# A decoder trunk on one core: the last gates' weights ahead of the pages, and the output weights in the space of the head inputs

## The chip, the cores and the metric

The kernel runs on one core of one Trainium2 chip, in float32 throughout. The metric is device time in microseconds (us) of one execution; the time before is the median of three runs.

## What is computed

Two layers, A and B, are run with the same weights for a prompt of 512 rows and for a group of 8 sequences with 4 new rows each (32 "sample" rows). Layer A mixes by trailing means and a memory attention. Layer B, in which the change lies, has multi-head latent attention and a memory attention, both gated, one output projection and a final norm:

```python
z = h @ w_in_b[j]
c_q, gate_t, q_m, gate_m = jnp.split(z, [...], axis=-1)
tok = mla_mix(c_q, pos, ckv_all, krope_all, ...)
mem_o = mem_attend(q_m..., mem_k[l], mem_v[l])
mixed = jnp.concatenate([tok * silu(gate_t), mem_o * silu(gate_m)], axis=-1)
x = x + mixed @ w_out[l]
return rmsnorm(x, g_final), ...
```

For the prompt the attention is causal over 512 rows, head by head (8 heads of 128). For the sample rows it goes over 4096 cached rows per sequence, in pages of 128 rows of 320 numbers (256 latent, 64 rotary) that a page table names, and over the 4 new rows themselves. `gate_t` has 1024 columns (8 blocks of 128), `mixed` has 1536 (12 blocks), `w_out` is 1536x1024.

## The kernel before

Activations lie transposed: 128 columns of the model on the partitions, 544 rows (512 prompt and 32 sample) along them, worked in two halves of 272. A product in float32 is made of three matmuls on numbers rounded to a shorter float (`mm3`, L93 to L95; `mm3_late`, L99 to L101): each factor is split into a high part, cast by ACT (L88), and the rest, a subtraction (L89) on DVE or POOL. A weight block goes `wr` (as loaded, L208) to `wh` and `wl`. The pool `pw` holds three `wr` and two of each of `wh` and `wl`.

PE is the engine with most work. From the late gates on, PE's and SP's instructions run in the order in which the code issues them. That order comes from `weave`: it steps through a few generators ("threads"), always the one that is furthest behind its planned share. ACT, DVE and POOL are ordered by the scheduler.

The parts from there on, in time:

- `gates_late`: the gates of blocks 4 to 7 of `gate_t`, 48 matmuls of 128x272 each (`pa` and `po` are the halves' sums). Woven with it are the first rounds of the pages. `late_w` holds the loaded weights. The split is issued in the gate that uses it. The loads of blocks 4 and 5 are issued early, block 6 behind the first 16 pages, block 7 behind 32.
- Rounds (`round_scores`, `round_values`): each of the 8 sequences has 2 rounds of 16 pages. `load_half` reads eight page numbers into registers (L973) and issues eight page loads (L977, `nat`, four buffers) on SP. PE transposes the keys (L134, `tr`, copied to `kt` at L985), makes scores (L1020 with the latent part, L1029 with the rotary one), and takes the values (L1057, after `rt`).
- `heads` and `head_inputs`: the prompt's eight heads, woven with the rounds. Their inputs (`qh`, `ql`, `wuh`, `wul`, `kx`, `qr`, `q`), raw weights and probabilities are in one pool, `pat`.
- `out_all`: the output projection of the prompt. Twelve slabs (two column halves `fh` times six steps `s`) of `w_out` (128x2x512 each, L1446) are loaded and split by `prepare`; a slab has 24 matmuls of 128x512 into four banks `oa`. `mix_b` makes the split of a gated block of `mixed`: from SBUF for blocks 0 to 7, from DRAM (`gmd`, the memory outputs) for 8 to 11. `load_rest` issues the loads of the residual `x` and the last gains on POOL. The pool `fin`, opened when `pat` closes, holds both slabs and `x`.
- `sample_out`, woven with the second part of `out_all`: `combine` joins the rounds' partial results with the 4 own rows (the own scores are L1292 and L1295, tiny matmuls), then the sample rows' output projection (L1541) reads the same `w_out` slabs again (`ws`, three buffers).

The first three slabs are split on DVE, later ones on POOL:

```python
wh, wl = split(fin("wh", F32R), fin("wl", F32R), t, nc.gpsimd if (fh, s) > (0, 2) else nc.vector)
```

Of the kernel before, what the change touches and what calls it, by code (L numbers as in the profile page):

```python
# [37 lines left out]
def trunk_kernel(ctx: ExitStack, tc: tile.TileContext, A, O):  # L38
# [891 lines left out]
    def weave(threads, last):  # L930

        while not all(t.done for t in last):
# [349 lines left out]
    weave([rv, rs, ha, hi], [ha, hi])  # L1282
    pat.close()
    hb.close()


    def combine(cb):
        ps = ps_("tr")
        sv = ps[:NS, :NS].rearrange("p (b t) -> p b t", b=NB)
        for b in range(NB):  # L1290
            for k in range(2):
                nc.tensor.matmul(  # L1292
                    sv[:, b, :], lhsT=QT[:, k, b, :], rhs=ckT_s[:, k, b * NT : (b + 1) * NT], start=k == 0, stop=False
                )
            nc.tensor.matmul(  # L1295
                sv[:, b, :], lhsT=Qr[:64, b, 0, :], rhs=krT_s[:, b * NT : (b + 1) * NT], start=False, stop=True
            )
        w = cb("c")
        tail = w[:NS, :NS].rearrange("p (b t) -> p b t", b=NB)
        nc.vector.tensor_tensor(  # L1300
            out=tail,
            in0=sv,
            in1=cp[:NS, C_TMASK : C_TMASK + NT].unsqueeze(1).broadcast_to([NS, NB, NT]),
            op=ALU.add,
        )
        tst = w[:NS, 64:80]
        nc.vector.tensor_reduce(out=tst[:, :NB], in_=tail, axis=AX.X, op=ALU.max, negate=True)
        nc.vector.tensor_tensor(out=tail, in0=tail, in1=tst[:, :NB].unsqueeze(2).broadcast_to([NS, NB, NT]), op=ALU.add)
        nc.scalar.activation(w[:NS, :NS], w[:NS, :NS], AF.Exp)
        nc.vector.tensor_reduce(out=tst[:, NB:], in_=tail, axis=AX.X, op=ALU.add)  # L1310
        L = P + NS
        yield 0.5, 4.5
        ps = ps_("tr")
        transpose(ps[:NB, :P], stats_m)
        transpose(ps[:NB, P:L], tst[:, :NB], NS)
        transpose(ps[:NB, L : L + P], stats_s)
        transpose(ps[:NB, L + P : 2 * L], tst[:, NB:], NS)
        ms = cb("t")
        nc.vector.tensor_copy(ms[:NB, : 2 * L], ps[:NB, : 2 * L])
        m, s = ms[:NB, :L], ms[:NB, L : 2 * L]  # L1320
        m3 = m.rearrange("p (g c) -> p g c", c=NS)
        g = cb("c")
        mn, den, rec = (g[:NB, i * NS : (i + 1) * NS] for i in range(3))
        nc.vector.tensor_reduce(out=mn, in_=m.rearrange("p (g c) -> p c g", c=NS), axis=AX.X, op=ALU.min)
        nc.vector.tensor_tensor(out=m3, in0=mn.unsqueeze(1).broadcast_to([NB, 5, NS]), in1=m3, op=ALU.subtract)
        nc.scalar.activation(m, m, AF.Exp)
        nc.vector.tensor_tensor(out=s, in0=s, in1=m, op=ALU.mult)
        nc.vector.tensor_reduce(out=den, in_=s.rearrange("p (g c) -> p c g", c=NS), axis=AX.X, op=ALU.add)
        nc.vector.reciprocal(out=rec, in_=den)
        nc.vector.tensor_tensor(out=m3, in0=m3, in1=rec.unsqueeze(1).broadcast_to([NB, 5, NS]), op=ALU.mult)  # L1330
        yield 0.5, 4.5
        ps = ps_("tr")
        transpose(ps[:, :NB], m[:, :P], NB)
        transpose(ps[:NS, 16 : 16 + NB], m[:, P:L], NB)
        wn = cb("c")
        nc.vector.tensor_copy(wn[:, :NB], ps[:, :NB])
        nc.vector.tensor_copy(wn[:NS, 16 : 16 + NB], ps[:NS, 16 : 16 + NB])
        selw = cb("t")
        nc.vector.tensor_tensor(
            out=selw[:, :256].rearrange("p (c t) -> p c t", c=NB),  # L1340
            in0=sel.unsqueeze(1).broadcast_to([P, NB, NS]),
            in1=wn[:, :NB].unsqueeze(2).broadcast_to([P, NB, NS]),
            op=ALU.mult,
        )
        tz = cb("t")
        nc.vector.memset(tz[:NS, :288], 0.0)
        nc.vector.tensor_tensor(
            out=tz[:NS, :288].rearrange("p (b c) -> p b c", c=36)[:, :, :NT],
            in0=tail,
            in1=wn[:NS, 16 : 16 + NB].unsqueeze(2).broadcast_to([NS, NB, NT]),  # L1350
            op=ALU.mult,
        )
        yield 0.5, 4.5
        ps = ps_("tr")
        for b in range(NB):
            transpose(ps[:NS, b * NS : (b + 1) * NS], tz[:NS, b * NS : (b + 1) * NS], NS)
        tt = cb("t")
        nc.vector.tensor_copy(tt[:NS, :256], ps[:NS, :256])
        yield 0.5, 4.5
        po = ps_("tr")  # L1360
        for bq in range(2):
            for r in range(2):
                for b4 in range(4):
                    b = bq * 4 + b4
                    if r == 0:
                        lhsT, rhs = selw[:, b * NS : (b + 1) * NS], ostore[:, b, :]
                    else:
                        lhsT, rhs = tt[:NS, b * NS : (b + 1) * NS], ck_nat
                    nc.tensor.matmul(
                        po[b4 * NS : (b4 + 1) * NS, bq * 256 : (bq + 1) * 256],  # L1370
                        lhsT=lhsT,
                        rhs=rhs,
                        start=r == 0,
                        stop=r == 1,
                    )
        on = cb("t")
        nc.vector.tensor_copy(on, po)
        yield 0.5, 4.5
        ps = ps_("tr")
        for i in range(4):  # L1380
            transpose(ps[:, i * P : (i + 1) * P], on[:, i * P : (i + 1) * P])
        oT = cb("t")
        for bq in range(2):
            for k in range(2):
                c = (bq * 2 + k) * P
                nc.vector.tensor_copy(
                    oT[:, k * 256 : (k + 1) * 256].rearrange("p (h b t) -> p b h t", h=8, b=NB)[
                        :, bq * 4 : bq * 4 + 4
                    ],
                    ps[:, c : c + P].rearrange("p (b h t) -> p b h t", b=4, h=8),  # L1390
                )
        v = [cb("v") for k in range(2)]
        for k in range(2):
            src = A["w_v_up"][k * P : (k + 1) * P].rearrange("p h c -> p (h c)")
            tc.keep_in_program_order(nc.sync.dma_start(v[k], src))
        yield 0.5, 4.5
        po = ps_("tr")
        for h2 in range(2):
            for k in range(2):
                for j in range(4):  # L1400
                    h = h2 * 4 + j
                    nc.tensor.matmul(
                        po[j * NS : (j + 1) * NS, h2 * P : (h2 + 1) * P],
                        lhsT=oT[:, k * 256 + h * NS : k * 256 + (h + 1) * NS],
                        rhs=v[k][:, h * P : (h + 1) * P],
                        start=k == 0,
                        stop=k == 1,
                    )
        ov = cb("t")
        nc.vector.tensor_copy(ov[:, :256], po[:, :256])  # L1410
        yield 0.5, 4.5
# [287 lines left out]
```

## Time and profile before

| | |
|---|---|
| median of three runs | 892.81 us (890.89 to 894.15) |
| profiled execution | 890.33 us, of which span 888.6 |
| mean granted TensorE clock | 0.984 |
| PE busy | 831.5 us, 94% of the span |
| DVE, ACT, POOL busy | 515.5, 349.5, 250.0 us (58, 39, 28%) |
| DMA | 139.46 MB, mean 157 GB/s |
| chain that ended last | PE 71%, DVE 10%, issue 6%, DMA 5%, ACT 4% |

The profile is of one execution; times in it count from the span's start. A row of its timeline reads: start, duration, engine, line and operation, what it writes and reads, and in brackets how long the engine had been idle and what released it. SPq stands for SP issuing a DMA; the transfer lands some microseconds later. A row of its table by stage has for each engine the busy time and the number of instructions, then the granted clock of PE (1.00 is full), the busy share of the DMA engines and GB/s. Busy PE may still be PE at half clock, which only the clock's column tells.

### The profile page before, as it was taken

The numbers are of one execution on the slowest core, as the hardware profiler recorded it, in microseconds if no ns is written. First come the engines' busy times: TensorE is split into PE (matmuls) and PEld (weight loads), VectorE is DVE, ScalarE is ACT, GpSimd is POOL, SyncE is SP. The second block draws the span as 40 slices with busy tenths as digits, with TensorE's granted clock in tenths as the row PEclk, the third lists the DMA queues.
The fourth block names the chain that finished last, engine by engine and source line by source line (L and its number), as shares of the span: only waits on it lengthen the run. The fifth ranks groups of instructions, "written<-read, shape, count | busy, mean of one in ns | idle before, by whom it ended". The sixth has DMA issues, their size and how long they took to land.

```text
span 888.6 us, 18551 instructions
## 1 busy us (share of the span) xinstructions
PE 831.5 (94%) x7162; PEld 715.1 (80%) x7162; DVE 515.5 (58%) x964; ACT 349.5 (39%) x693; POOL 250.0 (28%) x203
## 2 busy tenths in 40 slices
PE   6999999889999999999999789989999899899996
PEld 6989989889999898779988766768778777666664
DVE  7666666987734456757665225575656656544312
ACT  7443333222433253353332225544545535432212
POOL 0043323533334134024232127240411300032420
PEclk9999999999999999999999889999999999998998
DMA  8355176321232436366265725646555455792344
GB/s 303 96 196 185 48 246 204 105 69 52 100 106 84 119 123 201 98 213 223 77 222 187 210 90 179 201 148 179 161 166 175 138 148 159 239 326 70 119 143 171
DMA packets 80858, 139.46 MB, mean 157 GB/s; under 512 B 9057, under 2 KB 49762, under 8 KB 80514
## 3 DMA queue, kind: packets, MB, share of 16 engines
q1 hardware_dynamic: 76258, 123.53, 44.1%
q0 software_dynamic: 4512, 14.75, 4.7%
q8 instruction: 56, 0.92, 0.4%
q14 instruction: 32, 0.26, 0.1%
HBM read 129.53 MB, written 8.72 MB: 156 GB/s over the span
## 4 chain that ended last, share of the span: by engine, by line
PE 71%; DVE 10%; issue 6%; DMA 5%; ACT 4%; POOL 2%; SPq 2%; POOLq 0%; DVEq 0%; ACTq 0%
PE pa L93 13%; PE pa L95 13%; PE pa L94 13%; PE tr L134 7%; PE ac L1020 3%; PE ac L1057 3%; POOL wl L89 2%; DVE v L582 2%; PE oa L93 2%; PE ac L1029 1%; PE oa L94 1%; PE oa L95 1%; SPq L977 1%; DVE t L744 1%; PE ac L388 1%
## 5 line engine op out<-in xcount | busy, mean ns | idle before, releaser
L93 PE MATMUL pa<-h,wh 128*128 128x272 f32 x832 | 242.0, 293 | 9.7 <-ACT wh L88 5.2
L95 PE MATMUL pa<-h,wl 128*128 128x272 f32 x832 | 239.6, 293 | 5.1 <-POOL wl L89 5.1
L89 POOL TENSOR_TENSOR wl<-wr,wh 128x1024 fp32r<-128x1024 f32 (+1 forms) x64 | 148.7, 2324 | 247.9 <-ACT wh L88 234.0
L94 PE MATMUL pa<-h,wh 128*128 128x272 f32 x640 | 186.0, 291 | 0.0
L93 PEld LDWEIGHTS pa<-h,wh 128*128 128x128 f32 x832 | 158.9, 191 | 14.4 <-ACT wh L88 5.7
L95 PEld LDWEIGHTS pa<-h,wl 128*128 128x128 f32 x832 | 157.7, 191 | 7.9 <-POOL wl L89 6.2
L88 ACT CAST wh<-wr 128x1024 fp32r<-128x1024 f32 (+1 forms) x87 | 87.7, 1008 | 165.7 <-PE pa L94 53.8
L94 PEld LDWEIGHTS pa<-h,wh 128*128 128x128 f32 x640 | 122.8, 192 | 0.9
L134 PE MATMUL tr<-c,nat 128*128 128x128 f32 x512 | 79.6, 280 | 8.1 <-DVE kt L987 3.9
L985 ACT COPY kt<-tr 128x512 f32<-128x512 f32 x86 | 50.2, 588 | 72.1 <-PE tr L134 70.6
L134 PEld LDWEIGHTS tr<-c,nat 128*128 128x128 f32 x512 | 59.3, 141 | 23.4 <-issue 7.3
L260 DVE SCALAR_TENSOR_TENSOR g<-t,g 128x272 f32<-128x272 f32 x48 | 48.0, 1006 | 17.1 <-ACT t L259 17.1
L94 PE MATMUL pa<-g,wh 128*128 128x272 f32 x192 | 54.5, 288 | 0.1
L259 ACT ACTIVATE t<-g 128x272 f32<-128x272 f32 x48 | 20.3, 429 | 75.8 <-DVE g L246 74.5
L987 DVE COPY kt<-tr 128x512 f32<-128x512 f32 x42 | 28.9, 687 | 26.9 <-PE tr L134 26.6
L246 DVE SCALAR_TENSOR_TENSOR g<-pa,r 128x272 f32<-128x272 f32 x42 | 18.1, 438 | 43.3 <-PE pa L95 43.2
L93 PE MATMUL oa<-wh,c 128*128 128x512 f32 x96 | 41.5, 432 | 0.0
L94 PE MATMUL oa<-wl,c 128*128 128x512 f32 x96 | 38.8, 405 | 0.6 <-POOL wl L89 0.6
L94 PEld LDWEIGHTS pa<-g,wh 128*128 128x128 f32 x192 | 36.1, 188 | 0.3 <-DVE g L89 0.3
L89 DVE TENSOR_TENSOR wl<-wr,wh 128x1024 fp32r<-128x1024 f32 x23 | 28.1, 1224 | 12.7 <-ACT wh L88 12.6
L1020 PE MATMUL ac<-kt,c 128*32 128x256 f32 x512 | 34.9, 384 | 0.0
L89 DVE TENSOR_TENSOR q<-q,q 128x512 fp32r<-128x512 f32 x16 | 25.2, 1574 | 11.2 <-ACT q L88 11.1
(365 smaller groups left out, 1710.9 us busy)
## 6 DMA issues: line engine op xcount, KB each, us to landing
nat<-in_cache_P SPq DMA_DIRECT2D x256, 160.0 KB, 3.1
wr<-in_w_in_a SPq DMA_DIRECT2D x24, 512.0 KB, 3.8
wr<-in_w_in_b SPq DMA_DIRECT2D x19, 512.0 KB, 3.7
cs<-in_mem_kT SPq DMA_DIRECT2D x16, 512.0 KB, 5.4
wr<-in_w_out_a SPq DMA_DIRECT2D x16, 384.0 KB, 3.1
wr<-in_w_out_b SPq DMA_DIRECT2D x12, 512.0 KB, 5.5
ws<-in_w_out_b SPq DMA_DIRECT2D x12, 512.0 KB, 4.9
wr<-in_w_mem_k SPq DMA_DIRECT2D x8, 512.0 KB, 3.8
```

What stands on the lines that cost most here:

```text
L88: nc.scalar.copy(h, src)
L89: (eng or nc.vector).tensor_tensor(out=l, in0=src, in1=fr(h), op=ALU.subtract)
L93: nc.tensor.matmul(out, lhsT=wh, rhs=xh, start=start, stop=False)
L94: nc.tensor.matmul(out, lhsT=wh, rhs=xl, start=False, stop=False)
L95: nc.tensor.matmul(out, lhsT=wl, rhs=xh, start=False, stop=stop)
L134: nc.tensor.transpose(out, in_, ident[:k, :k])
L259: nc.scalar.activation(th[:, :HALF], z[:, o : o + HALF], AF.Tanh)
L260: nc.vector.scalar_tensor_tensor(out=z[:, o : o + HALF], in0=th[:, :HALF], scalar=1.0, in1=z[:, o : o + HALF], op0=ALU.add, op1=ALU.mult,)
L985: nc.scalar.copy(out, src)
L987: nc.vector.tensor_copy(out, src)
L1020: nc.tensor.matmul(o[j * NS : (j + 1) * NS, :], lhsT=QT[:, k, b, :], rhs=kt[ih, j // 2, k][:, j % 2 * 256 : (j % 2 + 1) * 256], start=k == ...
L1057: nc.tensor.matmul(po[j * NS : (j + 1) * NS, :256], lhsT=pT[:, i * P + j * NS : i * P + (j + 1) * NS], rhs=nat[i // 2][:, 2 * j + i % 2, : ...
```

## The change

Three things are done.

1. **Late gates.** Blocks 6 and 7 of the weights are loaded ahead of all pages, and a block's split is issued when the gate before it begins (`late_s`).
2. **Pools.** `pat` becomes three pools: `heads_raw`, `heads_val` and `heads_in`. `heads_in` closes as soon as the last head is scored (`weave` may now end on a condition), while its values are still to be made. `fin`, now only `wr`, `wh` and `wl`, takes that space. `x` and the gains go to `fin2`, in the place of the pages' pool when that closes. Small tiles of the last part use tags of the remaining pools.
3. **Output stage.** All slabs are split on POOL. The own scores become a thread of their own (`own_scores`), woven with the last head's values. `prepare` of the next slabs follows each finished slab; only step 4 is put off to be done together with step 5 (before: 3 and 4). The own `ws` slabs have five buffers, and their matmuls come two slabs at a time. The blocks 8 to 11 are read into `tab`.

```diff
     def gates_late():
         for f in range(4, 8):
-            wh, wl = split_w(late_w.pop(0), KD, P, nc.gpsimd)
-            if f == 4:
-                late_w.append(load_w(wb[3 + 7], KD, P)[0])
+            wh, wl = late_s.pop(0)
+            if late_w:
+                late_s.append(split_w(late_w.pop(0), KD, P, nc.gpsimd))
...
-    late_w = [load_w(wb[3 + f], KD, P)[0] for f in (4, 5)]
-    load_half(0, 0)
-    load_half(0, 1)
-    late_w.append(load_w(wb[3 + 6], KD, P)[0])
-    for h in range(2, 4):
+    late_w = [load_w(wb[3 + f], KD, P)[0] for f in (4, 5, 6)]
+    late_s = [split_w(late_w.pop(0), KD, P, nc.gpsimd)]
+    late_w.append(load_w(wb[3 + 7], KD, P)[0])
+    for h in range(4):
         load_half(h // 2, h % 2)
...
-    pat = Pool(
-        "pat", "left", tab=(512, 2), qw=(384, 2), qh=(384, 2), ql=(384, 2), wu=(512, 2), wuh=(512, 2), wul=(512, 2),
-        vx=(D, 2), kx=(512, 4), qr=(512, 3), e0=(128, 1), e1=(256, 1), e2=(384, 1), e3=(512, 1), p=(512, 4), q=(512, 5),
+    heads_raw = Pool("hraw", "left", tab=(512, 2), qw=(384, 2), wu=(512, 2))
+    heads_val = Pool("hval", "left", e0=(128, 1), e1=(256, 1), e2=(384, 1), e3=(512, 1), p=(512, 4), vx=(D, 2))
+    heads_in = Pool(
+        "hin", "left", qh=(384, 2), ql=(384, 2), wuh=(512, 2), wul=(512, 2), kx=(512, 4), qr=(512, 3), q=(512, 5)
     )
...
-    weave([rv, rs, ha, hi], [ha, hi])
-    pat.close()
-    hb.close()
...
+    weave([rv, rs, ha, hi], lambda: hi.done and heads_scored[0] == 8)
+    heads_in.close()
+    fin = Pool("fin", "left", wr=(D, 3), wh=(D, 3), wl=(D, 3))
...
+        wh, wl = split(fin("wh", F32R), fin("wl", F32R), t, nc.gpsimd)
...
+    prepared = [prepare(*slabs.pop(0)) for _ in range(3)]
...
         late = []
         for s in range(6):
-            if fh == 0 and s == 2:
-                load_rest()
-            if slabs:
-                prepared.append(prepare(*slabs.pop(0)))
             wh, wl = prepared.pop(0)
             late.append((s, wh, wl))
-            if s in (3, 4):
+            if s == 4:
                 continue
...
+            for _ in late:
+                if slabs:
+                    prepared.append(prepare(*slabs.pop(0)))
             late = []
...
+    os_ = Thread(own_scores(), 1.0, 0.0, 1.0, now[0])
+    weave([rv, rs, ha, os_], [ha, os_])
+    hb.close()
+    hb = Banks(oa=4)
+    out = Thread(out_all(), 112 / total, 66 / total, 66.0, now[0])
+    weave([rv, rs, out], [rv, rs])
+    sp_order.__exit__(None, None, None)
+    nats.close()
+    fin2 = Pool("fin2", "right", x=(D, 4), g=(D, 1), gs=(256, 1))
+    cb = Pool("cb", "right", c=(96, 3), ws=(D, 5))
+    load_rest()
...
-    out = Thread(out_all(), 118 / total, 66 / total, 66.0, now[0] + 10.0)
-    weave([rv, rs, out], [rv, rs])
-    sp_order.__exit__(None, None, None)
-    nats.close()
-    cb = Pool("cb", "right", v=(D, 2), t=(512, 4), c=(96, 3), ws=(D, 3))
...
-        here = [slab(cb("ws"), *todo.pop(0)) for _ in range(3)]
+        here = [slab(cb("ws"), *todo.pop(0)) for _ in range(5)]
...
-                yield 0.44, 1.0
+                if s % 2:
+                    yield 0.88, 0.5
```

PE issues as many instructions as before. The numbers in a name count tiles; they differ between the two programs for the same thing. Where the instructions stand, at the three places that matter below:

SP at the late gates, before: `p` is the last memory values, `nat` a half round of pages, `wr_5777` the weights of gate 6.

```order
L425 DMA p_5545<-in_cache_mem_v 128x512
L425 DMA p_5546<-in_cache_mem_v 128x512
L425 DMA p_5557<-in_cache_mem_v 128x512
L425 DMA p_5558<-in_cache_mem_v 128x512
L977 ISA
L977 DMA nat_5613<-in_cache_P 128x320
...
L977 DMA nat_5695<-in_cache_P 128x320
L208 DMA wr_5777<-in_w_in_b 128x1024
L973 TENSOR_LOAD c_4072
L973 ISA x16
```

The same place after, where `wr_5613` is gate 6's weights and `wr_5619` gate 7's; a line number is one higher there.

```order
L208 DMA wr_5613<-in_w_in_b 128x1024
L425 DMA p_5545<-in_cache_mem_v 128x512
L208 DMA wr_5619<-in_w_in_b 128x1024
L974 TENSOR_LOAD c_4072
L974 ISA x4
L425 DMA p_5546<-in_cache_mem_v 128x512
L425 DMA p_5557<-in_cache_mem_v 128x512
L974 ISA x2
L425 DMA p_5558<-in_cache_mem_v 128x512
L974 ISA x10
L978 ISA
L978 DMA nat_5621<-in_cache_P 128x320
```

Both loads moved ahead of 32 page loads and stand among the `p` loads. ACT in the same place, before: L259 is the tanh of a gate, `wh_6094` the cast of gate 6's weights.

```order
L259 ACTIVATE t_5976<-g_5949 128x272
L259 ACTIVATE t_6005<-g_5949 128x272
L985 COPY kt_6048<-tr_6043 128x512
L259 ACTIVATE t_6040<-g_6013 128x272
L985 COPY kt_6068<-tr_6063 128x512
L88 CAST wh_6094<-wr_5777 128x1024
```

And after, `wh_6013` for gate 6 and `wh_6098` for gate 7:

```order
L259 ACTIVATE t_5980<-g_5953 128x272
L88 CAST wh_6013<-wr_5613 128x1024
L259 ACTIVATE t_6009<-g_5953 128x272
L986 COPY kt_6052<-tr_6047 128x512
L259 ACTIVATE t_6044<-g_6017 128x272
L986 COPY kt_6072<-tr_6067 128x512
L88 CAST wh_6098<-wr_5619 128x1024
```

Gate 6's cast moved between the two tanh of gate 4, gate 7's into the place of gate 6's.

PE at the start of the output stage, before: `po` is the last head's values, `oa` the output.

```order
L101 MATMUL po_11677<-p_11758,vx_10662 128x128
L134 MATMUL tr_11862<-c_79,nat_11534 128x128 x4
L134 MATMUL tr_11869<-c_79,nat_11534 128x128 x4
L1020 MATMUL ac_11761<-kt_11753,c_4069 32x256 x2
L1020 MATMUL ac_11761<-kt_11804,c_4069 32x256 x2
L1020 MATMUL ac_11761<-kt_11867,c_4069 32x256 x2
L1020 MATMUL ac_11761<-kt_11874,c_4069 32x256 x2
L1029 MATMUL ac_11761<-nat_11534,c_4070 32x2x64 x8
L134 MATMUL tr_11897<-c_79,rt_11895 128x128 x4
L93 MATMUL oa_11904<-wh_11830,c_11820 128x512
```

And after, first the own scores' beginning ahead of the last head's values (L1401 and L1404, which are eight pairs), then the start of the output stage:

```order
L1244 MATMUL hs_11631<-c_3828,qr_9904 128x512
L134 MATMUL tr_11646<-c_79,nat_11172 128x128 x4
L1401 MATMUL tr_11701<-c_3814,c_4069 32x4 x2
L1404 MATMUL tr_11701<-c_3815,c_4070 32x4
...
L134 MATMUL tr_11884<-c_79,nat_11540 128x128 x4
L99 MATMUL po_11762<-p_11842,vx_10668 128x128
L100 MATMUL po_11762<-p_11842,vx_10669 128x128
L101 MATMUL po_11762<-p_11843,vx_10668 128x128
L93 MATMUL oa_11899<-wh_11669,c_11659 128x512
```

The output's first matmul now follows the last head's values at once; two groups of transposes, the last scores and the transposes of `rt` moved behind it. PE's order between the gates and the last head's scores is the same in both.

POOL in the output stage, before, where the first three slabs' subtractions are on DVE:

```order
L1431 DMA m_11914<-gmd 128x512
L1464 DMA x_12060<-x1d 128x1024
L1464 DMA x_12062<-x1d 128x1024
L1464 DMA x_12064<-x1d 128x1024
L1464 DMA x_12066<-x1d 128x1024
L1467 DMA g_12068<-in_g_final 128x1024
L1470 DMA gs_12070<-in_g_final 32x2x128 x4
L1431 DMA m_11976<-gmd 128x512
L1431 DMA m_11982<-gmd 128x512
L89 TENSOR_TENSOR wl_11923<-wr_11920,wh_11922 128x1024
```

And after, up to the loads of `x`:

```order
L1297 DMA tab_11989<-gmd 128x512
L89 TENSOR_TENSOR wl_11670<-wr_11667,wh_11669 128x1024
L89 TENSOR_TENSOR wl_11684<-wr_11681,wh_11683 128x1024
L89 TENSOR_TENSOR wl_11698<-wr_11695,wh_11697 128x1024
L89 TENSOR_TENSOR wl_11942<-wr_11939,wh_11941 128x1024
L89 TENSOR_TENSOR wl_11998<-wr_11995,wh_11997 128x1024
L89 TENSOR_TENSOR wl_12057<-wr_12054,wh_12056 128x1024
L1330 DMA x_12119<-x1d 128x1024
L1330 DMA x_12121<-x1d 128x1024
```

The reads of `gmd` moved ahead of all slabs, the loads of `x` behind six subtractions.

More of the change, by code (lines that the diff above doesn't have):

```diff
@@ L930, in weave @@
     def weave(threads, last):
-        while not all(t.done for t in last):
+        through = last if callable(last) else lambda: all(t.done for t in last)
+        while not through():
             can = [
@@ L1281, in trunk_kernel @@
     ha = Thread(heads(), 24 / total, 94 / total, 46.0, now[0])
-    weave([rv, rs, ha, hi], [ha, hi])
-    pat.close()
-    hb.close()
[L1287 to L1411, printed above, removed]
-        ps = ps_("tr")
-        for h2 in range(2):
-            transpose(ps[:, h2 * P : (h2 + 1) * P], ov[:, h2 * P : (h2 + 1) * P])
-        for h in range(8):
-            nc.vector.tensor_tensor(
-                out=gs[:, h, :], in0=ps[:, h * NS : (h + 1) * NS], in1=gs[:, h, :], op=ALU.mult
-            )
-        yield 0.5, 1.0
@@ L1477, in out_rows @@
         pts = [ps_("oa") for _ in range(4)]
+        pts = [pts[j] for j in (0, 3, 1, 2)]
         def run(s, j, wh, wl):
@@ L1523, in out_all, with own_scores @@
         yield from out_rows(1)
-    out = Thread(out_all(), 118 / total, 66 / total, 66.0, now[0] + 10.0)
+    own = []
+    def own_scores():
+        ps = ps_("tr")
+        sv = ps[:NS, :NS].rearrange("p (b t) -> p b t", b=NB)
+        for b in range(NB):
+            for k in range(2):
+                nc.tensor.matmul(
+                    sv[:, b, :], lhsT=QT[:, k, b, :], rhs=ckT_s[:, k, b * NT : (b + 1) * NT], start=k == 0, stop=False
+                )
+            nc.tensor.matmul(
+                sv[:, b, :], lhsT=Qr[:64, b, 0, :], rhs=krT_s[:, b * NT : (b + 1) * NT], start=False, stop=True
+            )
+        w = pat("qw")
+        tail = w[:NS, :NS].rearrange("p (b t) -> p b t", b=NB)
+        nc.vector.tensor_tensor(
+            out=tail,
+            in0=sv,
+            in1=cp[:NS, C_TMASK : C_TMASK + NT].unsqueeze(1).broadcast_to([NS, NB, NT]),
+            op=ALU.add,
+        )
+        tst = w[:NS, 64:80]
+        nc.vector.tensor_reduce(out=tst[:, :NB], in_=tail, axis=AX.X, op=ALU.max, negate=True)
+        nc.vector.tensor_tensor(out=tail, in0=tail, in1=tst[:, :NB].unsqueeze(2).broadcast_to([NS, NB, NT]), op=ALU.add)
+        nc.scalar.activation(w[:NS, :NS], w[:NS, :NS], AF.Exp)
+        nc.vector.tensor_reduce(out=tst[:, NB:], in_=tail, axis=AX.X, op=ALU.add)
+        own.extend([tail, tst])
+        yield 0.5, 0.0
+    os_ = Thread(own_scores(), 1.0, 0.0, 1.0, now[0])
[3 more added lines that the diff above has]
+    out = Thread(out_all(), 112 / total, 66 / total, 66.0, now[0])
     weave([rv, rs, out], [rv, rs])
@@ L1569, in trunk_kernel @@
     pe_order.__exit__(None, None, None)
-    for p in (cb, pro, pg, pc, fin, pt, pr, small):
+    for p in (cb, fin2, pro, pg, pc, fin, heads_val, heads_raw, pt, pr, small):
         p.close()
```

133 lines of the change are left out of this document (121 added, 12 removed).

## The prediction, made before the changed kernel was run

> **What bounds the kernel now.** I read the page's busy shares first, then one table by stage, then PE's list of waits, then the instructions around the longest of them. PE bounds: 831.5 of 888.6 us. A saving here is time in which PE waits or in which its clock is halved, since PE issues the same matmuls after the change. Four stages of the table: gates 4 and 5, gates 6 and 7, the rounds of pages with the heads (to the last head's last score at 764.3), and, after a transition of 21.6 us, the output stage:
> ```profile
> PE 831.5 (94%) x7162; PEld 715.1 (80%) x7162; DVE 515.5 (58%) x964; ACT 349.5 (39%) x693; POOL 250.0 (28%) x203
> ...
> core 0: us, PE busy (x) PEld busy (x) DVE busy (x) ACT busy (x) POOL busy (x), PEclk, DMA share, GB/s
> ...
> 483.80:497.10 13.30, 13.30 (x109) 13.30 (x109) 3.46 (x12) 2.37 (x5) 0.65 (x4) 1.00 0.74 212
> 497.10:529.60 32.50, 23.36 (x183) 21.06 (x182) 8.41 (x14) 6.35 (x12) 7.16 (x6) 0.79 0.50 152
> 529.60:764.30 234.70, 223.28 (x2372) 172.67 (x2371) 143.90 (x324) 117.35 (x271) 57.96 (x56) 1.00 0.55 163
> ...
> 785.90:879.80 93.90, 91.41 (x647) 65.62 (x646) 29.91 (x70) 22.36 (x41) 24.64 (x14) 0.96 0.47 160
> ```
> The worst stretch is the second: PE idles 9.14 us of 32.5, at a granted clock of 0.79. The first, the same work for gates 4 and 5, has neither idle time nor a lowered clock. PE's waits after 483 us (total, times, longest), the instructions of gate 6, and the two half-clock windows (length, PE busy, clock):
> ```profile
> PE pa L93 <- ACT wh L88: 5.2, 2, 3.2
> PE pa L95 <- POOL wl L89: 3.9, 2, 2.0
> ...
> PE tr L134 <- DMA nat<-in_cache_P: 2.7, 3, 1.3
> ...
> 494.44 0.37 SPq L208 DMA_DIRECT2D wr<-in_w_in_b  x1
> 499.50 1.04 ACT L88 CAST wh<-wr 128x1024 fp32r<-128x1024 f32 x1 [3.40 <-DMA wr<-in_w_in_b]
> 500.60 0.39 PE L93 MATMUL pa<-h,wh 128*128 128x272 f32 x1 [3.23 <-ACT wh L88]
> 500.68 2.35 POOL L89 TENSOR_TENSOR wl<-wr,wh 128x1024 fp32r<-128x1024 f32 x1 [15.67 <-ACT wh L88]
> ...
> 500.60:508.00 7.40, 5.44 (x24) 0.54 0.69 206
> 516.60:525.20 8.60, 6.59 (x29) 0.60 0.35 109
> ```
> Gate 6's weights are issued at 494.44, behind 16 page loads. Only when they land does the chain of cast, first matmul, subtraction, third matmul begin, and PE stands twice, for wh and for wl. Gate 7 repeats it, and the clock falls after each.
>
> **The change, part by part.**
>
> A. Late gates. Both weights go ahead of all pages on SP and each split is issued a gate ahead. The four waits go: 5.2 + 3.9 = 9.1 us, all of the stage's idle time. The half clock follows these gaps, so it goes with them: the clock is short by 0.46 x 7.4 + 0.40 x 8.6 = 6.8 us in the two windows, of which at most half of their idle time (1.96 and 2.01) fell where nothing ran: 4.9. Will the splits be ready? wh and wl have two buffers, so gate 6's split waits for gate 4's matmuls (they end at about 490) and gate 7's for gate 5's (497.1). Cast 1.04 and subtraction 2.35 make 3.4, a gate takes 6.6 (two in 13.3), so both are ready some 3 us early. POOL's subtractions lie beside DVE's gate work, which has room: 3.5 of 13.3 busy. A = 14.0, bounds 12 and 14.6.
>
> The two loads now stand on SP ahead of the last memory values (p) and of every page:
> ```profile
> 472.59 4.70 SPq L425 DMA_DIRECT2D p<-in_cache_mem_v  x4
> ...
> 481.86 1.06 PE L428 MATMUL ac<-p,z 128*32 128x128 f32 x32
> 482.76 11.58 SPq L977 DMA_DIRECT2D nat<-in_cache_P  x16
> ```
> The four p issues span 4.70 us, since they wait for buffers; two issues of 0.37 fit between. But a megabyte more is on the way beside them, and L428 reads p 5 us after the last of them. Bounds 0 and 2; I take 0.3. The first page is issued only when L428 is through, so the loads don't delay it. Sixteen pages take SP 11.6 plus some 2.7 of register loads, about 7 us a half, so the four halves land by about 490, 497, 504 and 511; PE, without its waits, wants the second at about 500, the third at 512, the fourth at 515. Margin 3 us at the nearest.
>
> B. Rounds and heads, 234.7 us. PE's order is the same, so it shifts whole. Into head 7's time come four casts and four subtractions of 128x512 (the memory outputs times their gates), by half of the slab's cast (1.05) and subtraction (1.23, below) some 0.6 each, 4.5 us together. DVE is busy 143.9 and ACT 117.4 of 234.7, so most falls into free time. Bounds 0 and 2.5; I take 0.7.
>
> C. From the last score to the end: the slabs of output weights, the first matmuls and the own scores.
> ```profile
> 773.70 2.05 SPq L1446 DMA_DIRECT2D wr<-in_w_out_b  x3
> ...
> DMA to landing us min/median/max: 6.9/6.9/6.9
> ...
> 784.78 1.23 DVE L89 TENSOR_TENSOR wl<-wr,wh 128x1024 fp32r<-128x1024 f32 x1
> ...
> 785.91 0.48 PE L93 MATMUL oa<-wh,c 128*128 128x512 f32 x1
> 786.23 0.39 PE L94 MATMUL oa<-wl,c 128*128 128x512 f32 x1
> 786.46 0.40 PE L95 MATMUL oa<-wh,g 128*128 128x512 f32 x1
> ...
> 795.40 2.34 POOL L89 TENSOR_TENSOR wl<-wr,wh 128x1024 fp32r<-128x1024 f32 x1 [3.72 <-ACT wh L88]
> ...
> 795.47 0.29 PE L1292 MATMUL tr<-c,c 128*32 128x4 f32 x4
> ...
> 798.53 0.79 PE L93 MATMUL oa<-wh,c 128*128 128x512 f32 x1
> ```
> C1. The own scores (795.47 to 798.53, 3.0 us of tiny matmuls) move to where PE waits 2.7 us for pages, so they are nearly free. The output stage starts with its first split slab: issued at 773.70 behind the last pages, as before, landed 6.9 later at 780.6, cast 1.05, and now POOL's 2.34 where DVE took 1.23: 784.1 against 785.91. PE is there at about 781 and stands some 2.8 us. The 12 transposes and 16 small matmuls that stood ahead of 785.91 come later, some 2.5 us. So 3.0 + 1.8 − 2.5 = 2.3 (bounds 0 and 4.8).
>
> C2. That stand of 2.8 is new, and the waits of 2.0 above were followed by half clock. One such window, 3.4 us (798.1, below), costs half of it less what falls in the stand: C2 = −1.5, bounds −3 and 0. The Trainium skill, TensorE: Matmul & The Clock Gate, Part 1: The HAM clock gate, says that the clock falls after at least one idle window, about 3.4 us; by it C2 would be 0. The rows here show the fall after shorter stands, so I keep −1.5.
>
> C3. Stalls and half clock in the output stage:
> ```profile
> 798.10:801.50 3.40, 3.40 (x14) 0.50 0.78 272
> 812.20:821.40 9.20, 7.60 (x28) 0.81 0.19 60
> ...
> 811.89 2.38 POOL L89 TENSOR_TENSOR wl<-wr,wh 128x1024 fp32r<-128x1024 f32 x1 [3.97 <-ACT wh L88]
> 812.48 2.07 DVE L1339 TENSOR_TENSOR t<-c,c 128x256 f32<-128x256 f32 x1
> 815.21 0.79 PE L95 MATMUL oa<-wh,t 128*128 128x512 f32 x1 [1.60 <-DVE t L89]
> 815.80 0.63 PE L93 MATMUL oa<-wh,c 128*128 128x512 f32 x1
> 816.23 0.63 PE L94 MATMUL oa<-wl,c 128*128 128x512 f32 x1
> 835.04 0.50 PE L94 MATMUL oa<-wl,c 128*128 128x512 f32 x1 [0.63 <-POOL wl L89]
> ```
> At full clock a matmul follows the last by 0.23 (786.23, 786.46), a slab's 24 take 5.6. After the own scores the clock is at half for 3.4, of which 1.4 is lost in the slab. The window from 812.2 takes 9.2: 3.6 lost, because the memory outputs' subtractions stand on DVE behind L1339, which takes 2.07 beside POOL's subtraction. At 835.04 a third slab split late costs 0.63 and the restart about 0.3. The change hoists those subtractions, moves the own scores, and prepares a slab after each slab. C3 = 1.4 + 3.6 + 0.9 = 5.9, bounds 3 and 6.6.
>
> C4. The sample rows' output matmuls come in 6 groups, not 12. After a change of shape the second oa matmul follows by 0.32 (785.91 to 786.23), 0.09 more than 0.23; a group changes twice, 0.19. Five or six fewer: 1.0, bounds 0 and 1.3.
>
> C5. The end, and the row block before the last:
> ```profile
> 875.07 0.69 DVE L1488 TENSOR_TENSOR x<-oa,x 128x512 f32<-128x512 f32 x1 [3.51 <-PE oa L95]
> 878.80 0.38 SPq L1501 DMA_DIRECT2D out_y_p<-x  x1
> ...
> 880.01 0.69 DVE L1488 TENSOR_TENSOR x<-oa,x 128x512 f32<-128x512 f32 x1 [1.64 <-PE oa L95]
> 881.95 2.63 SPq L1562 DMA_DIRECT2D out_y_s<-c  x4
> 885.31 0.38 SPq L1501 DMA_DIRECT2D out_y_p<-x  x1
> ```
> From its last addition to its last issue the end takes 5.3, the block before it 3.7, because four stores of the sample rows stand ahead on SP. They now come ahead of all others. C5 = 1.5, bounds 1 and 1.6.
>
> Sum: 14.0 − 0.3 − 0.7 + 2.3 − 1.5 + 5.9 + 1.0 + 1.5 = 22.2 us. The profiled execution took 890.3, so 868.1 beside it; the median of the three runs, 892.8, stands 2.5 above, and I forecast 870.5.
>
> **The rivals.**
>
> R1, pages. If a half costs SP more than 7 us, or the weights on the way slow the pages, PE stands for nat where it stood for weights, and the clock falls again: A's 14.0 given back, 884. For it: a margin of 3 us. Against it: 2.7 us of page waits in the whole list.
>
> R2, the output stage keeps its losses. POOL alone splits every slab, and the x loads, which wait for the pages' space, stand between two splits on it; a slab later than 5.6 us after the one before stops PE. C1, C2 and C3 together (6.7) would then come to about −2: 879. For it: 835.04. Against it: 12 x 2.34 = 28 us of POOL in 94. The Trainium skill, SBUF — State Buffer, Who interferes with whom, says that a DVE operation with two SBUF inputs contends with a GpSimd one that reads there, and one blocks for a whole instruction. L1339's 2.07 us beside POOL agrees.
>
> R3, slower. The stand before the output stage starts a half clock that lasts. Then a matmul follows by 0.43 (815.80, 816.23), 0.20 more, and 24 x 12 = 288 of them add 57: 926 with C2 counted once. The gain is gone from 22.2 / 0.20 = 111 matmuls at half. Against it: the half-clock stretches shown lasted 3.4 to 6.9 us.
>
> R4, the stand of 2.8 us is too short to lower the clock, C2 = 0: 869. By the clock page's rule it is.
>
> R5, the splits aren't ahead, because buffers come free later than I read. Then wl's 3.9, two casts and the half clock, 4.9, stay: 881.
>
> **How the numbers follow.** Forecast as summed 0.56, R4 0.16, R1 0.09, R2 0.12, R3 0.03, R5 0.03, no change 0.01. The range reaches down to 864 (A, C1 and C3 at their upper ends and C2 at 0 make 5.3, some 1 more from B and p) and up to 881 (R2 and R5 inside, R1 and R3 outside). Changes under 0.3%, 2.7 us, can't be told from none here. Faster takes the forecast, R4, R5, R1 and R2 less a little for their meeting, 0.95; the same 0.02; slower 0.03.
>
> **What the profile after should show.** A: no wait of PE for wh or wl in gates 5 to 7, clock 1.00 there, gate 7's end at about 516. C1: own scores inside the page wait, first oa matmul some 3.5 us after the slab lands. C2: half clock right behind it. C3: no slab above 6 us. C5: about 7 us from the last matmul to the end. I am wrong if PE waits for nat, or if POOL's splits come late behind x loads.

## The result, and the profile after

The changed kernel takes 865.64 us (median of 4 runs, 864.47 to 867.66) against 892.12 (890.89 to 894.15): ratio 0.9703, 95% interval 0.9677 to 0.9730, or 24 to 29 us less. The profiled execution took 867.66, its span 865.8; it is the longest of the four, which matters below. The same two views as before, first the busy shares and the table by stage (cut at the same instructions: first and last late gate, last head's last score, first and last matmul of the output stage), then PE's waits from 470 us on:

```profile
PE 823.7 (95%) x7162; PEld 711.3 (82%) x7162; DVE 514.9 (59%) x961; ACT 349.9 (40%) x693; POOL 257.9 (30%) x206
...
486.00:499.30 13.30, 13.30 (x108) 13.30 (x109) 5.30 (x12) 3.63 (x7) 3.03 (x5) 1.00 0.68 199
499.30:517.30 18.00, 18.00 (x188) 16.62 (x187) 8.37 (x14) 5.39 (x11) 4.86 (x5) 1.00 0.72 227
517.30:752.20 234.90, 223.71 (x2369) 172.30 (x2367) 146.00 (x328) 119.18 (x274) 60.05 (x60) 1.00 0.56 167
752.20:769.70 17.50, 17.46 (x207) 13.20 (x205) 7.10 (x17) 8.19 (x18) 0.78 (x1) 0.90 0.73 230
769.70:857.50 87.80, 86.14 (x645) 63.79 (x644) 27.48 (x63) 21.52 (x39) 35.75 (x25) 1.00 0.51 181
857.50:865.80 8.30, 0.22 (x1) 0.00 (x0) 2.41 (x5) 2.17 (x4) 0.55 (x1) 0.75 0.42 155
```

```profile
PE tr L134 <- DVE kt L988: 3.9, 4, 1.7
...
PE oa L94 <- POOL wl L89: 1.1, 1, 1.1
...
PE ac L1558 <- DMA ws<-in_w_out_b: 0.6, 2, 0.4
...
PE tr L134 <- DMA nat<-in_cache_P: 0.3, 2, 0.2
```

Gates 6 and 7 take 18.0 us where they took 32.5: PE has no idle time and full clock there, and no wait for wh or wl of the gates is left in the list. The rounds with the heads take the same 235. The transition shrank from 21.6 to 17.5, and PE works through it, at a granted clock of 0.90. The output stage takes 87.8 where it took 93.9. Only the end is nearly as long as it was. The waits for pages in the transition are gone (2.0 us before, none after; in the whole list 2.7 and 0.3), and one is new: 1.1 us for the first slab's wl.

The place of that wait, by what ACT, POOL and SP do there, and the clock in the 3.4 us that begin with the output stage's first matmul:

```profile
758.00 3.94 SPq L978 DMA_DIRECT2D nat<-in_cache_P  x8
762.04 9.64 SPq L1312 DMA_DIRECT2D wr<-in_w_out_b  x4
...
767.73 1.05 ACT L88 CAST wh<-wr 128x1024 fp32r<-128x1024 f32 x1 [1.53 <-DMA wr<-in_w_out_b]
768.92 7.54 POOL L89 TENSOR_TENSOR wl<-wr,wh 128x1024 fp32r<-128x1024 f32 x3 [32.12 <-ACT wh L88]
...
769.70:773.10 3.40, 2.30 (x12) 1.00 0.14 41
```

The slab is issued behind the last pages at 762.04, its cast starts at 767.73, its subtraction ends at 771.3. PE stands 1.1 us, not the 2.8 that I forecast, and the clock stays at 1.00 behind it.

### The profile page after: what moved, and what is told of

It is laid out like the page before. It is cut to its first block, busy times and chain, and to the rows that moved or that the text cites. A ratio compares the mean times of both kernels' runs of the same rounds, so it can differ in the third digit from the quotient of the medians.

```text
span 865.8 us, 18559 instructions
## 1 busy us (share of the span) xinstructions
PE 823.7 (95%) x7162; PEld 711.3 (82%) x7162; DVE 514.9 (59%) x961; ACT 349.9 (40%) x693; POOL 257.9 (30%) x206
## 4 chain that ended last, share of the span: by engine, by line
PE 51%; issue 7%; DVE 6%; DMA 3%; ACT 3%; SPq 1%; POOL 1%; POOLq 0%; ACTq 0%; DVEq 0%
PE pa L93 8%; PE pa L95 8%; PE pa L94 8%; PE tr L134 6%; PE oa L93 2%; PE ac L1021 2%; PE oa L94 2%; PE oa L95 2%; PE ac L1058 2%; PE ac L1030 1%; DVE t L744 1%; DMA wr<-in_w_mem_v 1%; SPq L978 1%; DMA ws<-in_w_out_b 1%; DMA wr<-in_w_out_b 1%
## 5 line engine op out<-in xcount | busy, mean ns | idle before, releaser
L89 POOL TENSOR_TENSOR wl<-wr,wh 128x1024 fp32r<-128x1024 f32 (+1 forms) x67 | 156.5, 2337 | 249.6 <-ACT wh L88 233.0
L260 DVE SCALAR_TENSOR_TENSOR g<-t,g 128x272 f32<-128x272 f32 x48 | 50.0, 1048 | 14.4 <-ACT t L259 14.2
L259 ACT ACTIVATE t<-g 128x272 f32<-128x272 f32 x48 | 20.3, 429 | 73.0 <-DVE g L246 71.7
L89 DVE TENSOR_TENSOR wl<-wr,wh 128x1024 fp32r<-128x1024 f32 x20 | 24.5, 1224 | 12.8 <-ACT wh L88 12.7
```

Source lines behind the costliest of these rows:

```text
L89: (eng or nc.vector).tensor_tensor(out=l, in0=src, in1=fr(h), op=ALU.subtract)
L259: nc.scalar.activation(th[:, :HALF], z[:, o : o + HALF], AF.Tanh)
L260: nc.vector.scalar_tensor_tensor(out=z[:, o : o + HALF], in0=th[:, :HALF], scalar=1.0, in1=z[:, o : o + HALF], op0=ALU.add, op1=ALU.mult,)
```

## The experiments

All times are medians beside runs of the kernel before on the same chip (medians 892.1 to 892.3). The changed kernel was run twice more with its own profile, so there are three of it.

**The late loads alone.**

```diff
-            wh, wl = split_w(late_w.pop(0), KD, P, nc.gpsimd)
...
+            wh, wl = late_s.pop(0) if f == 4 else split_w(late_w.pop(0), KD, P, nc.gpsimd)
...
-    late_w = [load_w(wb[3 + f], KD, P)[0] for f in (4, 5)]
-    load_half(0, 0)
...
+    late_w = [load_w(wb[3 + f], KD, P)[0] for f in (4, 5, 6)]
+    late_s = [split_w(late_w.pop(0), KD, P, nc.gpsimd)]
+    late_w.append(load_w(wb[3 + 7], KD, P)[0])
...
```

> The kernel before with only the two late weights issued ahead of the pages; the splits stay written in the gate that uses them, and the scheduler puts them in the very places that it gives them in the changed kernel. Theory (the place of the loads is the whole of the first part): 14 to 15 us less than before, about 877.5, PE without a wait for wh or wl in gates 5 to 7, clock 1.00 there. Rival (issuing a split a gate ahead is needed): the two waits for the subtraction, two casts and the half clock stay, 11 us, so only some 3 to 4 us less, about 888.

876.43 us, ratio 0.9815 (0.9791 to 0.9839), 16 us less than before. The two stages of the gates in its table:

```profile
484.60:497.80 13.20, 13.20 (x108) 13.20 (x108) 5.29 (x12) 3.60 (x7) 3.05 (x5) 1.00 0.68 200
497.80:515.80 18.00, 18.00 (x188) 16.62 (x187) 8.38 (x14) 5.42 (x11) 4.85 (x5) 1.00 0.72 227
```

They are those of the changed kernel. The loads' place is the whole of the first part. Writing a split a gate ahead adds nothing to that: in this run, where the splits are written in their gates, the instructions of every engine from 440 us to the last gate's end stand in the same order as in the changed kernel, so with the loads early the scheduler puts the splits there itself. The opposite, splits written ahead with the loads late, was not run.

**The output stage alone.** The changed kernel with `gates_late` and the loads as before.

> The changed kernel with the late gates' loads put back as they were before. Theory (the two parts add up, since PE's order between them is the same): the gates' waits of 9 us and their half clock are back, so 14 to 15 us more than the changed kernel and 10 to 11.5 less than before, about 881. Rival (the output stage gains only because PE comes to it earlier): less than 6 us below before, 886 or more.

882.28 us, ratio 0.9870 (0.9839 to 0.9901), 10 us less than before. PE's waits for the gates' weights are back:

```profile
PE pa L93 <- ACT wh L88: 5.4, 2, 3.4
PE pa L95 <- POOL wl L89: 3.9, 2, 2.0
...
PE oa L94 <- POOL wl L89: 2.0, 1, 2.0
```

The parts add up: 16 and 10 against 26 for both. The rival, under 6, is out.

**The changed kernel again.**

> The changed kernel once more, as it is. In its first profile PE stood longer at 345 us, in code that the change does not touch, and came out 2.3 us later there than before; theory (chance, from one execution to the next): in this profile the gap at that place is another one, and against the kernel before all other offsets come out as in the first profile within 1 us. Rival (the change causes it): the same 2.3 us again. Time about 865.6.

866.81 us. The stretch from 344 to 354 us, which lies before everything that was edited, in the kernel before, in the first profile of the changed kernel and in this one:

```profile
344.00:354.00 10.00, 8.72 (x68) 1.00 0.42 128
```

```profile
344.00:354.00 10.00, 7.96 (x49) 0.83 0.31 112
```

```profile
344.00:354.00 10.00, 9.17 (x74) 1.00 0.37 117
```

In the first profile PE did 49 matmuls there, at a clock of 0.83, and 68 and 74 in the others. The last matmul of L428, just ahead of gate 4, started at 484.85 us in the first profile of the changed kernel, at 484.04 and 482.59 in the two later ones, at 482.64 in the kernel before. So the 2.2 us by which the first profile came late to the gates are chance, and the profile's 22.7 us of gain stand beside 26.5 of the medians. At the start of the output stage this execution differs as well:

```profile
PE oa L94 <- POOL wl L89: 2.0, 1, 2.0
PE oa L93 <- ACT wh L88: 0.4, 1, 0.4
...
767.80:773.30 5.50, 3.45 (x8) 0.72 0.34 113
```

PE came to it earlier, stood 2.4 us, and half clock followed.

**The first slab's subtraction on DVE.**

```diff
-        wh, wl = split(fin("wh", F32R), fin("wl", F32R), t, nc.gpsimd)
+        wh, wl = split(fin("wh", F32R), fin("wl", F32R), t, nc.gpsimd if (fh, s) > (0, 0) else nc.vector)
```

> The changed kernel with the first slab's subtraction on DVE (1.23 us) and not on POOL (2.34). Theory (the stand of 1.1 us for wl at the first matmuls of the output stage is POOL's longer subtraction): the wait goes, 1 us less than the changed kernel. Rival (DVE is still at the last head's probabilities and the pages' copies there): its subtraction comes as late or delays those, no gain or up to 1 us more.

866.53 us, the changed kernel's time. PE's waits and the clock at the start:

```profile
PE oa L93 <- ACT wh L88: 1.0, 1, 1.0
PE oa L94 <- DVE wl L89: 0.8, 1, 0.8
...
768.60:773.50 4.90, 4.11 (x10) 0.65 0.52 178
```

The wait for wl fell to 0.8, but the stand as a whole was 1.8 and half clock came behind it. The theory's microsecond is there, and the gain is not: from the slab's landing to the second output matmul, the first that needs wl, it is 2.4 us where the changed kernel's three profiles have 3.6. But the slab landed 16.7 us behind the last score, where those have 15.8 to 16.1, and PE stood for that landing. Where the subtraction runs can't be told from the time.

**The first slab ahead of the last eight pages.**

```diff
-    prepared = [prepare(*slabs.pop(0)) for _ in range(3)]
+    prepared = [prepare(*slabs.pop(0))]
+    slab_out.append(True)
+    for half in held:
+        load_half(*half)
+    prepared.extend([prepare(*slabs.pop(0)) for _ in range(2)])
...
-                    load_half(n + 4 // 2, i // 2)
+                    if (n + 4 // 2, i // 2) == (len(rounds) - 1, 1) and not slab_out:
+                        held.append((n + 4 // 2, i // 2))
+                    else:
+                        load_half(n + 4 // 2, i // 2)
```

> The changed kernel with the first slab of output weights issued on SP ahead of the last eight page loads, right after the last head's last score. Theory (the output stage's start hangs on the landing of the first slab, which stands behind those pages): it lands some 5 us earlier, the wait for wl of 1.1 to 2.4 us at the first matmuls goes and with it the half clock that followed it in two of three profiles, 2 to 3 us less than the changed kernel, about 863.5. Rival (the pages, now behind the slab, become late instead): PE waits for nat by 1 to 3 us more, no gain.

865.76 us, ratio 0.9701 (0.9668 to 0.9733): in the time no difference. In the trace the mechanism is as the theory has it:

```profile
754.30 0.39 SPq L1317 DMA_DIRECT2D wr<-in_w_out_b  x1
757.56 3.95 SPq L978 DMA_DIRECT2D nat<-in_cache_P  x8
...
760.67 2.38 POOL L89 TENSOR_TENSOR wl<-wr,wh 128x1024 fp32r<-128x1024 f32 x1 [25.36 <-ACT wh L88]
...
769.80:773.00 3.20, 3.20 (x16) 1.00 0.12 37
```

The subtraction ends at 763.0, PE starts without a wait at full clock. From the first to the last matmul of the output stage it is 85.6 us, where the changed kernel's three profiles have 87.5, 89.4 and 87.5. Of this, 1.1 us were lost ahead of it (19.0 from the last score to the first output matmul, against 17.2 to 17.9; the run with both small edits, below, has 17.9). The rest, some 1 to 2 us, is less than three rounds can tell.

**The own scores back in the output stage.**

```diff
-    os_ = Thread(own_scores(), 1.0, 0.0, 1.0, now[0])
-    weave([rv, rs, ha, os_], [ha, os_])
+    weave([rv, rs, ha], [ha])
...
     def combine(cb, v):
+        yield from own_scores()
         tail, tst = own
```

> The changed kernel with the own scores back at the start of the joining of the sample rows, behind the start of the output stage. Theory (in the page wait they are nearly free): PE waits 2.5 us for pages again and does the own scores 3 us later in the output stage with half clock behind them, 1.4; the half clock ahead, 1.2, goes: 3 us more than the changed kernel. Rival (they cost there what they cost here): within 1 us of the changed kernel.

873.94 us, ratio 0.9783 (0.9747 to 0.9819), 7 to 8 us above the changed kernel, more than either theory had. PE's waits at the start of the output stage, and the clock from there:

```profile
PE oa L93 <- ACT wh L88: 2.5, 1, 2.5
PE oa L94 <- POOL wl L89: 2.0, 1, 2.0
...
767.90:776.50 8.60, 6.58 (x18) 0.60 0.66 242
```

The first output matmul comes no earlier (18.45 us behind the last score, against 17.85), since the slab's landing sets it, which was late in this execution (17.3 us behind the last score, against 15.8 to 16.1). PE stands 4.5 us, with half clock behind, and then does the own scores in the output stage, again with half clock behind (0.50 from 802.5 to 805.9). That stage takes 95.6 us. So the own scores cost next to nothing where the change put them: PE waited there for the slab as well as for pages.

**The end: the root on ACT and DVE, and more work on POOL.** The profile after: the last row block, and POOL's drain, an entry (DRAIN) of POOL at the end of the program. One drain is long (5253 ns), two are short:

```profile
857.76 0.69 DVE L1355 TENSOR_TENSOR x<-oa,x 128x512 f32<-128x512 f32 x1 [0.89 <-PE oa L95]
...
861.48 0.38 SPq L1368 DMA_DIRECT2D out_y_p<-x  x1
...
L1698 POOLq DRAIN  x3: 51/107/5253, 859.7 to 865.5; - x3
```

The last store is issued 3.7 us behind the last addition, as forecast, and lands after 2.3 us, at 863.75. POOL's drain begins with its last power at 859.7 and lasts 5.25 us, to 864.94; the end waits for it. In the kernel before the same drain ended at 887.47, with the last store's landing (887.57):

```profile
L1680 POOLq DRAIN  x3: 51/103/5250, 882.2 to 888.3; - x3
```

Two kernels put this to the test:

```diff
-            r = rstd_cols(sq, 1, P, D)
+            r = st(1)
+            nc.scalar.activation(r, sq, AF.Sqrt, scale=1.0 / D, bias=eps_c)
+            nc.vector.reciprocal(out=r, in_=r)
```

> The changed kernel, where the last rows' reciprocal root is made by a root on ACT (its table loaded once) and a reciprocal on DVE, and no longer by a power on POOL. In the profile after, POOL's last entry is a drain of 5.25 us right behind its last power, which ends 1.2 us after the last store landed. Theory (the end hangs on that drain): the drain comes earlier, the end follows the last store's landing by about 1.0 us as in the kernel before, 1.2 us less, and 0.3 more for a shorter chain: span from the last matmul's end to the end 8.3 us becomes about 6.8. Rival (the drain only fills time until another event): the span behind the last matmul stays above 8.

```diff
+            if j == 3:
+                for _ in range(6):
+                    nc.gpsimd.tensor_tensor(out=st(1), in0=r, in1=mhalf[:, :1], op=ALU.pow)
```

> The changed kernel with six more tiny powers on POOL behind the last one that is needed, each 0.55 us, off the stores' path. Theory (the end hangs on POOL's drain, which starts when POOL has nothing left to issue): the end moves by 3 to 3.5 us, from 8.3 to about 11.5 behind the last matmul. Rival (the end hangs on the stores): it stays at 8.3.

865.40 us for the first (0.9705, 0.9673 to 0.9736), which the time alone doesn't tell from the changed kernel, and 871.32 for the second (0.9765, 0.9726 to 0.9804; two runs). POOL's drains, of the first and of the second, with the added powers ahead:

```profile
L1703 POOLq DRAIN  x3: 51/107/5285, 844.2 to 860.8; - x3
```

```profile
860.53 3.21 POOL L1367 TENSOR_TENSOR s<-s,c 128x1 f32<-128x1 f32 x6
...
L1701 POOLq DRAIN  x3: 51/107/7902, 860.5 to 868.9; - x3
```

With the root off POOL its drain is over long before, and the end follows the last store's landing (860.03) by 1.0 us. From the last output matmul's start to the end it is 7.71 us instead of 8.44. Of the 1.2 us between the last landing and the drain's end 0.7 are gained: the chain up to the landing became 0.3 longer (6.7 against 6.4), where 0.3 less was expected, and the end stands 1.0 behind the landing and not 0.8 as behind the drain. With six more powers, which no store waits for, the end comes 3.3 us later, 11.73 behind that matmul. The drain ends 4.66 us behind POOL's last instruction in both the changed kernel (860.28) and this one (863.74). The end hangs on it; that is shown from both sides.

**Both small edits together, with the changed kernel beside them.**

> The changed kernel with both small edits: the first slab ahead of the last eight pages, and the last rows' root on ACT and DVE and not on POOL. From their profiles: the wait for wl at the start of the output stage and the half clock behind it gone (1 to 2 us), the end 0.7 us shorter; 2 to 2.5 us less than the changed kernel, about 863.5. Rival: the time of this stretch only moves to another wait, no difference from the changed kernel in the same call.

> The changed kernel once more, as the measure for the kernel beside it: 865.5 to 867, with a stand of 1 to 2.5 us for the first slab's wl and, by the theory that a stand of about 2 us is enough to halve the clock, half clock behind it where the stand is over 2 us and none where it is about 1.

864.07 us, ratio 0.9688 (0.9672 to 0.9705), and 866.19 us, 0.9716 (0.9698 to 0.9734). By the profiles 1.9 us less in the output stage and 0.7 at the end. The medians differ by 2.1, but the intervals overlap a little, so it is a likely gain and not a sure one. The changed kernel's third profile stood 1.4 us at the start, and the clock stayed at 1.00.

**Twelve groups again.**

```diff
-                if s % 2:
-                    yield 0.88, 0.5
+                yield 0.44, 1.0
```

> The changed kernel with the sample rows' output matmuls in 12 groups of 16 again. Theory (a group costs two changes of shape, 0.2 us): six more groups, 1 to 2 us more than the changed kernel, each group of 16 taking 0.57 us where a group of 32 takes 1.01. Rival (the groups are hidden by waits for ws): no difference.

867.41 us, 0.9740 (0.9713 to 0.9766): 1.2 us above the changed kernel beside it, which the intervals don't separate. A group and the matmuls behind it, in the changed kernel and in this one:

```profile
842.27 1.08 PE L1558 MATMUL ac<-ws,c 128*32 128x128 f32 x32
843.28 0.50 PE L93 MATMUL oa<-wh,c 128*128 128x512 f32 x1
```

```profile
847.70 0.65 PE L1558 MATMUL ac<-ws,c 128*32 128x128 f32 x16
848.28 0.50 PE L93 MATMUL oa<-wh,c 128*128 128x512 f32 x1
```

It is 1.01 us for 32 against 0.58 for 16, so two groups of 16 take 0.15 more than one of 32. To this comes a second change of shape there and back: the step into a group is 0.32 and the one out of it 0.34, where one 128x512 matmul follows another by 0.23. Together that is some 0.33 for a pair, 2 us for six. In the changed kernel's three profiles two of its six groups lost 0.4 to 1.0 of it again, beside waits for ws.

**The gated memory outputs late.**

```diff
-            t = pat("tab")
+            t = pat("vx", F32, SEQ)
             nc.gpsimd.dma_start(t, gmd[k - 8])
```

> The changed kernel, where the gated memory outputs (blocks 8 to 11) are read into the two tiles of the last head's values, so that their casts and subtractions can't start before that head is done, as they could not before the change. Theory (having them early is what took away the stand of 1.6 us and the half clock in the slab that reads them): some of the 3.6 us come back, 1.5 to 4 us more. Rival (their lateness before was DVE's queue beside POOL and not their buffers): they are ready in time all the same, since the slab comes 20 us behind that head, and nothing changes.

868.52 us, 0.9734 (0.9716 to 0.9753). Its first slabs, and a stretch in which the memory outputs are read:

```profile
768.10:781.30 13.20, 11.13 (x36) 0.74 0.47 163
799.40:806.70 7.30, 7.30 (x33) 1.00 1.01 373
```

The difference lies in the first slabs, where this execution stood 3.2 us (1.2 for wh, 2.0 for wl) with half clock behind. The stretch from 799.4 runs as in the changed kernel (7.2 us), and PE waits for no memory output. So in that slab it is the rival: the subtractions of the memory outputs end some 9 us ahead of their first use here and over 50 in the changed kernel, and the one is as good as the other. The median is 2.3 us above the changed kernel's beside it, with intervals that overlap a little; whether the long stand at the first slabs comes with this edit or is chance stays open. What the kernel before lacked was such a lead; whether its queue on DVE or its buffers took it is not told apart here.

## Why the prediction was right, and where it was off

The forecast was 870.5 with a range of 864 to 881, and faster with 0.95; 865.6 is inside, 5 us below the forecast: 26.5 us of gain where I summed 22.2. By terms, from the profiles:

- **A, 14.0 forecast.** From the last matmul of L428 to the last late gate's last matmul it was 47.35 us before and 32.29 in each of the three profiles after: 15.1. The mechanism was right, the half clock's share was mis-sized: 9.1 of waits, and 5.9 instead of 4.9. I subtracted half of the idle time as if all of it had fallen into half clock, but in gate 7 the clock was still 1.00 in the first 1.0 us of the wait for wl (517.2 to 518.2), which is half of the missing 1.0; the other half isn't accounted for. The page wait that R1 feared didn't come.
- **p, 0.3.** Measured 0: from the last gate matmul ahead of L428 to the last of L428 it is 3.4 us in the kernel before and in all three profiles after. What looked like a loss in the first profile was chance at 345 us.
- **B, 0.7.** Last gate to last score: 234.1 before, 234.8, 234.4 and 235.3 after. Mean 0.7 more, as taken.
- **C1 and C2.** From the last score to the first output matmul 21.8 became 17.2 to 17.9, some 4 us. But that matmul needs only wh, and the stand for wl comes behind it. To the second, which needs wl, 22.1 became 19.4 to 19.7: 2.5 to 2.7 where I had 1.8. Of the 2.7 us of page waits on which I put the own scores, 0.7 lay at 726 us, long before; the transition had 2.0. The step that failed is that PE would be at the start at 781, 16.9 us behind the last score, and wait for both halves of the slab. It was there at 16.8 in the second profile, and stood 0.4 for wh and 2.0 for wl. In the first and the third, half clock behind the own scores (756 to 759 us in the first, where the transition's clock is 0.90), a cost that the sum lacks, brought it there 1.0 later, and it stood 1.1 and 1.4. C2's half clock came in the second alone. In the others R4's outcome came, full clock, but at a shorter stand than its 2.8.
- **C3 and C4.** First to last output matmul: 93.7 before, 87.5, 89.4 and 87.5 after. By my terms (own scores 3.0 out, deferred work 2.5 in, C3 5.9, C4 1.0, less C2) it is 5.9 less; measured 4.3 to 6.2, the stand for wl included. C1 to C4 together, from the last score to the last output matmul, are 8.9 to 10.1 where the sum has 7.7.
- **C5, 1.5.** Measured 0.55: 8.99 became 8.44. The step that failed is that the end follows the last store. The stores did come 1.6 us earlier; POOL's drain, which had lain level with them, then set the end.
- **R2** did not come: POOL's 35.8 us of 87.8 kept ahead of the slabs, and no later slab waits for its wl. **R3** neither: every half-clock stretch ended. **R5** neither: PE has no wait for wh or wl in the gates.

Profiled executions give 24 to 25 us when the place at 345 us is left out; the medians 26.5, within the interval of 24 to 29.

The Trainium skill, TensorE: Matmul & The Clock Gate, Part 1: The HAM clock gate, has the clock fall after at least one idle window of about 3.4 us. The traces here don't agree. At the start of the output stage stands of 1.1, 1.3, 1.4 and 1.6 us (wl waits of the changed kernel twice, of the kernel with 12 groups, and of the one with the root on ACT) were followed by full clock, and stands of 1.8, 2.0, 2.4, 3.2 and 4.5 by half, the longest of them without a matmul in between 2.5 us. These lengths are no threshold either. The wait of 1.6 us for t, ahead of 815.21 in the kernel before, was followed by half clock (0.50 from 815.3 to 818.5), and the same wait of 1.6 us in the run with the late loads alone by full clock (1.00 from 802.6 to 806.0). A stand of 2.1 us at 197 us, ahead of all that was edited, was followed by half clock in the changed kernel's first two profiles (0.57 and 0.65 from 199 to 203) and by full clock in its third and in the kernel before (1.00).

## What to carry to other kernels

A load on an in-order queue is as late as what is written ahead of it: look for weights that stand behind bulk loads which nobody needs yet. Before moving code to have work done earlier, see whether the data's arrival or the code's place sets the time; here the scheduler needed only the load. Filler such as the own scores belongs where the critical engine waits anyway, and is worth more there than its own length, since a stand of about 2 us can cost the clock behind it too.

## What was not expected of the hardware

- POOL's drain at the end of the program lasts until 4.66 us behind its last instruction (before: power ended 882.81, drain 887.47; after: 860.28 and 864.94; with six more powers 863.74 and 868.40). An instruction of 0.55 us on POOL in the last row block can set the end of the kernel.
- At the start of the output stage the clock fell after stands of 1.8 us and more and not after 1.6 or less, in ten profiles. At other places a stand of the same length, 1.6 or 2.1 us, was followed by half clock in one execution and by full clock in another, so the length alone doesn't decide it.
- Code that was not touched moves the time of a profile by some us: the last matmul of L428 started between 480.2 and 485.2 us in 14 profiles of kernels that differ up to there at most in the place of two loads. Differences of 1 to 2 us are read from a stage, not from a span.
